# A decoder trunk on one core: the eight products of a weight tile in varying order

## The chip, the core and the metric

The kernel runs on one NeuronCore of a Trainium2 chip. TensorE (PE) multiplies; its weight loads (PEld) run beside its products. VectorE (DVE), ScalarE (ACT) and GpSimd (POOL) do elementwise work, SyncE (SP) issues most transfers. The metric is the device time of one execution in microseconds. Weights lie in HBM as float32. SBUF holds the tiles, PSUM (eight banks of 512 float32 columns by 128 partitions) the running sums.

## The reference

Two layers on 256 positions of width 2048, each a mixer and a gated MLP with a causal convolution, and a LayerNorm after each of them:

```python
h = x
mix = mamba2_mixer(h, mamba_w_in[0], ..., mamba_w_out[0])           # 2048 -> 10304, scan over 2 chunks, 4096 -> 2048
h = layer_norm(ALPHA * h + mix, ...)
h = layer_norm(ALPHA * h + conv_ffn(h, ffn_w_up[0], ..., ffn_w_down[0]), ...)   # 2048 -> 2 x 5632 -> 2048
k_blk, v_blk, k_mean = shared_kv(h, w_kv)                           # 2048 -> 4096
mix = moba_cross_attention(h, attn_w_q[0], attn_w_o[0], k_blk, v_blk, k_mean)   # 16 heads
h = layer_norm(ALPHA * h + mix, ...)
h = layer_norm(ALPHA * h + conv_ffn(h, ffn_w_up[1], ..., ffn_w_down[1]), ...)
```

Nearly all of the arithmetic is the products of the 256 positions with the large weight matrices. With 256 positions each weight is used for little work, so all weights pass through SBUF once.

## The kernel before

**Steps and chunks.** The weights are cut on the host into 881 tiles of 128 x 2 x 512 float32, half a megabyte each. One tile is one step (`steps`); a chunk (`Chunk`) is 512 columns of one weight matrix over its whole depth. The program is written out step by step at the end of `yoco_kernel`: for every step the functions hung before it, its products, then the functions hung after it. This order by hand sets the order on every engine.

**Two parts of each weight.** A float32 number is taken as the sum of a rounded part, `hi`, and the rest, `lo`, both in the type float32r. `split` (line 192) makes them: ACT casts the raw tile to `hi` (L223), DVE subtracts to get `lo` (L224), and then the load of a later tile is issued on SP's queue (L179). Four raw tiles and four tiles each of `hi` and `lo` exist. The activations are split in the same way: `hT` holds for each of 16 row blocks 256 columns of the high part and then 256 of the low one. `x.both(k)` is all 512, `x.hi(k)` the first 256.

**Where the tiles start.** `split` gives each kind of tile an offset in a row of `LINE` = 64 elements (lines 198 to 212). A plain `hi` tile has its two halves one right behind the other. A `hi` tile whose step is `behind` has 48 elements before its first half and 576 before its second. A `lo` tile of mode W has its halves 544 elements apart.

**Modes.** In mode W (560 steps: the Mamba input projection, most of both MLP up-projections, K and Q) the weights are TensorE's stationary operand, and the activations stream past them. In mode X (most of the rest) it is the other way round: the activations are stationary, the weights stream, and all products of a half of the positions add into one bank (`half`, L247, L248, L252); the last chunk of such a sum ends with products of 256 columns ("pieces"). One chunk has mode H (L289).

**The products of a W step** (`some`, line 258). A tile of a W chunk holds four row blocks of 256 columns. Its first index, `a`, is the part of the tile, `b` the row block within the part, `j` one of two 128-column pieces; numbered in the order (a, b, j), 0 to 3 lie in the first part and 4 to 7 in the second. `j` is also the PSUM bank that the product adds to. With p = 0 the weights are `hi` and 512 columns stream by (L275); with p = 1 they are `lo` and only the 256 high columns stream by (L278). In the first chunk of all a tile holds two row blocks of 512 columns, and `j` runs over four banks.

**Which comes first.** `whole` (line 293) issues the eight products of each kind. In the Mamba chunks each step has first one kind and then the other, and the next step begins with the kind that the last one ended with (`kinds`). In the others two steps are taken together: both with one kind, then both with the other. A step is `behind` (line 183) when its `hi` products follow `lo` products. The next tiles' splits are put into the stream after a fixed number of these products.

In the kernel before, the eight products with p = 0 go in the order 0 to 7, and the eight with p = 1 in the order 0, 1, 4, 5, 2, 3, 6, 7 (line 268). The first product of a bank in a chunk begins its sum, the last one ends it (`begins`, `ends`).

**Other work on TensorE.** L806 turns 128 x 128 tiles, L867 is a mean in two products of 256 columns, L823 and L832 belong to the scan.

Of the kernel before, what the change touches and what calls it, by code (L numbers as in the profile page):

```python
# [53 lines left out]
WARM0 = 18  # L54
HEAD, TAIL = 3, 4
LAST = 8
SPARE = 3


# [32 lines left out]
def yoco_kernel(ctx: ExitStack, tc: tile.TileContext, x, lmg, lmb, lfg, lfb, x_t, columns, w, out):  # L92
# [14 lines left out]
    def tp_tile():  # L107
        return psum.tile([P, NC], F32, tag="tp", name="tp", bufs=2)
# [73 lines left out]
    def behind(i):  # L182

        ch, s = steps[i]
        if ch.mode != "W" or (ch.paired and s % 2):
            return False
        if ch.kinds(s)[0] == 1:
            return True
        ch, s = steps[i - 1]
        return i > 0 and ch.mode == "W" and ch.kinds(s)[1] == 1  # L190
# [67 lines left out]
    def some(ch, s, p):  # L258

        i = ch.first + s  # L260
        nj = ch.nj
        w = ((hi_t, lo_t)[p][i]).rearrange("p a (k n) -> p a k n", n=nj * P)
        k0, half = ch.place(s)
        banks = [p[:, j, :] for p in ch.part[half:] for j in range(2)]
        first = ch.kinds(s)[0] == p
        order = [(a, b, j) for a in range(2) for b in range(ch.per // 2) for j in range(nj)]
        if p == 1:
            order = [order[i] for i in (0, 1, 4, 5, 2, 3, 6, 7)]
        for a, b, j in order:
            yield  # L270
            k = k0 + a * (ch.per // 2) + b
            begins, ends = first and k == 0, not first and k == ch.nk - 1
            js = slice(j * P, (j + 1) * P)
            if p == 0:
                nc.tensor.matmul(banks[j], w[:, a, b, js], ch.x.both(k), start=begins, stop=ends,  # L275
                                 skip_group_check=True)
            else:
                nc.tensor.matmul(banks[j][:, :S], w[:, a, b, js], ch.x.hi(k), start=begins, stop=ends,  # L278
                                 skip_group_check=True)
# [12 lines left out]
    def whole(i):  # L292

        ch, s = steps[i]
        if ch.mode == "H":
            return beside(i)
        a, b = ch.kinds(s)
        if not ch.paired:
            order = [(s, a), (s, b)]
        elif s % 2 == 0:  # L300
            order = [(s, a), (s + 1, a)]
        else:
            order = [(s - 1, b), (s, b)]
        late = ch.paired and s % 2
        n = len(order) * ch.per * ch.nj
        c = 0
        for t, p in order:
            for _ in some(ch, t, p):
                if c == (n // 2 if late else n * 3 // 8):
                    if late:  # L310
                        done(i - 1)
                    run(mid, i)
                    splits(i)
                c += 1
        if not ch.paired or late:
            done(i)

    def products(i):
# [6 lines left out]
        elif s == 0:  # L325
            a = acc_pair()
            ch.part = [a[:, 0, :], a[:, 1, :]] if ch.mode == "X" else [a]
            if ch.tail:
                if ch.tail == LAST:
                    ch.piece = [tp_tile()[:, :HC] for _ in range(2)]  # L330
# [49 lines left out]
    def beyond(i, t, q, f, *a):  # L380

        outer.setdefault((i, t, q), []).append((f, a))
# [168 lines left out]
    def summed(x, tail=TAIL):  # L551

        return [Chunk(Acts(x), tail=tail * (c == 3), head=2 * (c == 3)) for c in range(4)]

    def ffn_chunks(tail):
        return [(Chunk(hs, head=0 if j else HEAD), Chunk(hs)) for j in range(DFF // NC)], summed("g", tail)
# [7 lines left out]
    chA = summed("a")  # L564
    up1, down1 = ffn_chunks(LAST)
    n_steps = len(steps)
# [370 lines left out]
    def chain(norm, nxt=None, after=None):  # L937
# [16 lines left out]
        beyond(last, 1, 0, norm.scale, 0, 0)  # L954
        for e in range(SPARE):
            spare[last - SPARE + 1 + e] = 4 + 4 * e
        n = nxt.first
# [192 lines left out]
    for h in range(HEADS):  # L1150
        i, j = divmod(h, 4)
# [88 lines left out]
```

## Time and profile before

| | |
|---|---|
| median of two runs | 2505.25 us (2504.73 to 2505.77) |
| the profiled execution | 2505.77 us, its span 2503.5 us |
| clock granted to TensorE | 0.999 |
| TensorE busy | 2490.5 us, 99% of the span |
| weight loads busy | 2155.7 us, 86% |
| DVE, ACT, POOL busy | 1660.2, 1364.3, 76.4 us |
| DMA | 201 GB/s on average, 502.55 MB |

The span runs from the first instruction to the last; the time of the execution has some 2 us more around it. A product's recorded duration contains the time until its results are out and overlaps with the next product, so the pace of TensorE is read from the distance of starts, or from the lengths in the chain of waits, which follows the work that ended last back from the end and gives each piece its start, its length and the number of instructions in it.

### The profile page before, as it was taken

The page shows a single profiled execution, that of the slowest core. Times are in us where ns is not written, and L with a number is a line of the kernel's source. Part 1 is how long each engine was busy: PE and PEld are TensorE (multiplying, and loading weights), DVE is VectorE, ACT ScalarE, POOL GpSimd, SP SyncE. Part 2 cuts the span into 40 slices and gives each one's busy share as a digit, 9 for nine tenths or more (in the row PEclk, how much of TensorE's full clock was granted, in tenths as well). Part 3 has the DMA queues.
Part 4 walks back from the last instruction along what each step waited for, and adds up shares of the span by engine and source line. Part 5 has one row for each costly group of instructions (what it writes and reads, how often), then busy time and mean ns, then how long its engine had stood idle before and what let it go on. Part 6 is the DMA issues. An engine that isn't in the chain of part 4 may idle for free.

```text
span 2503.5 us, 35513 instructions
## 1 busy us (share of the span) xinstructions
PE 2490.5 (99%) x13695; PEld 2155.7 (86%) x13695; DVE 1660.2 (66%) x2144; ACT 1364.3 (54%) x1790; POOL 76.4 (3%) x96
## 2 busy tenths in 40 slices
PE   9999999999999999999999999999999999999998
PEld 8888888888888888888888888888888888888887
DVE  7778888855676767675445646645767676765545
ACT  6677787643465655554334445544556555554333
POOL 0000000000200000000000200000200000000001
PEclk9999999999999999999999999999999999999999
DMA  7666655666665555556676665457666555566675
GB/s 257 202 198 203 212 192 190 205 208 222 215 206 194 194 193 193 195 185 202 211 227 210 210 193 177 160 177 228 221 192 198 195 192 196 186 199 204 196 227 166
DMA packets 141738, 502.55 MB, mean 201 GB/s; under 512 B 15857, under 2 KB 16369, under 8 KB 141569
## 3 DMA queue, kind: packets, MB, share of 16 engines
q1 hardware_dynamic: 136448, 482.92, 59.0%
q0 software_dynamic: 4832, 16.85, 2.2%
q8 instruction: 107, 1.75, 0.3%
q14 instruction: 63, 0.51, 0.1%
q10 hardware_dynamic: 288, 0.52, 0.1%
HBM read 491.77 MB, written 8.45 MB: 200 GB/s over the span
## 4 chain that ended last, share of the span: by engine, by line
PE 98%; DMA 1%; DVE 0%; ACT 0%; issue 0%; SPq 0%; ACTq 0%; DVEq 0%
PE acc L275 41%; PE acc L278 20%; PE acc L247 11%; PE acc L252 11%; PE acc L248 11%; DMA raw<-in_w 1%; PE acc L823 1%; PE tp L419 0%; PE tp L832 0%; PE acc L806 0%; PE tp L1104 0%; PE tp L1138 0%; PE tp L1130 0%; PE tp L252 0%; PE tp L247 0%
## 5 line engine op out<-in xcount | busy, mean ns | idle before, releaser
L224 DVE TENSOR_TENSOR lo<-raw,hi 128x1024 fp32r<-128x1024 f32 (+1 forms) x869 | 1060.4, 1226 | 716.9 <-ACT hi L223 592.9
L223 ACT CAST hi<-raw 128x1024 fp32r<-128x1024 f32 (+1 forms) x869 | 907.9, 1048 | 822.1 <-PE acc L252 384.9
L275 PE MATMUL acc<-hT,hi 128*128 128x512 f32 x4480 | 1055.9, 391 | 1.2 <-ACT hi L223 1.2
L275 PEld LDWEIGHTS acc<-hT,hi 128*128 128x128 f32 x4480 | 826.6, 188 | 162.8 <-ACT hi L223 2.2
L278 PEld LDWEIGHTS acc<-hT,lo 128*128 128x128 f32 x4480 | 538.7, 188 | 15.6 <-issue 1.2
L278 PE MATMUL acc<-hT,lo 128*128 128x256 f32 x4480 | 544.4, 277 | 0.0
L247 PE MATMUL acc<-hi,gT 128*128 128x512 f32 (+1 forms) x670 | 260.5, 389 | 0.0
L248 PE MATMUL acc<-lo,gT 128*128 128x512 f32 (+1 forms) x670 | 260.3, 389 | 0.0
L252 PE MATMUL acc<-hi,gT 128*128 128x512 f32 (+1 forms) x670 | 206.0, 389 | 0.0
L248 PEld LDWEIGHTS acc<-lo,gT 128*128 128x128 f32 x670 | 125.8, 188 | 26.0
L247 PEld LDWEIGHTS acc<-hi,gT 128*128 128x128 f32 x670 | 125.8, 188 | 26.0 <-DVE r L473 0.3
L252 PEld LDWEIGHTS acc<-hi,gT 128*128 128x128 f32 x670 | 125.7, 188 | 25.9
L247 PE MATMUL acc<-hi,yT 128*128 128x512 f32 (+1 forms) x246 | 95.4, 388 | 0.0
L248 PE MATMUL acc<-lo,yT 128*128 128x512 f32 (+1 forms) x246 | 95.3, 388 | 0.0
L247 PE MATMUL acc<-hi,hT 128*128 128x512 f32 x192 | 78.8, 410 | 0.0
L248 PE MATMUL acc<-lo,hT 128*128 128x512 f32 x192 | 75.5, 393 | 0.0
L252 PE MATMUL acc<-hi,yT 128*128 128x512 f32 (+1 forms) x246 | 75.3, 388 | 0.0
L628 DVE TENSOR_TENSOR u<-u,acc 128x512 f32<-128x512 f32 x108 | 73.5, 682 | 2.4 <-ACT u L627 1.4
L655 DVE SCALAR_TENSOR_TENSOR g<-u,cols,g 128x254 f32<-128x254 f32 (+1 forms) x176 | 73.3, 478 | 2.1 <-ACT g L650 2.1
L1054 ACT CAST gT<-v 128x512 fp32r<-128x512 f32 x44 | 27.3, 621 | 84.6 <-DVE v L1053 84.6
L655 DVE SCALAR_TENSOR_TENSOR v<-u,cols,v 128x254 f32<-128x254 f32 (+1 forms) x176 | 73.1, 478 | 0.0
L486 POOL TENSOR_TENSOR rs<-rs,mhalf 128x1 f32<-128x1 f32 x8 | 7.4, 930 | 1975.5 <-DVE nb L487 1975.5
(224 smaller groups left out, 1824.7 us busy)
## 6 DMA issues: line engine op xcount, KB each, us to landing
raw<-in_w SPq DMA_DIRECT2D x880, 512.0 KB, 3.8
mA<-acum_d POOLq DMA_DIRECT2D x16, 512.0 KB, 6.7
hres<-r POOLq DMA_DIRECT2D x12, 512.0 KB, 7.1
r<-hres SPq DMA_DIRECT2D x12, 512.0 KB, 5.0
eA<-acum_d POOLq DMA_DIRECT2D x16, 128.0 KB, 7.9
r<-in_x SPq DMA_DIRECT2D x4, 512.0 KB, 5.5
gb<-in_ln_mix_g SPq DMA_DIRECT2D x8, 256.0 KB, 4.9
gb<-in_ln_mix_b SPq DMA_DIRECT2D x8, 256.0 KB, 5.1
```

Source lines behind the costliest of these rows:

```text
L223: nc.scalar.copy(h[:, sl], t[:, sl])
L224: nc.vector.tensor_sub(l[:, sl], t[:, sl], h[:, sl].bitcast(F32))
L247: nc.tensor.matmul(a, th, h[:, kk, sl], start=k == k0, stop=False)
L248: nc.tensor.matmul(a, th, l[:, kk, sl], start=False, stop=False)
L252: nc.tensor.matmul(a, ch.x.lo(k)[:, ts], h[:, kk, sl], start=False, stop=k == k1 - 1)
L275: nc.tensor.matmul(banks[j], w[:, a, b, js], ch.x.both(k), start=begins, stop=ends, skip_group_check=True)
L278: nc.tensor.matmul(banks[j][:, :S], w[:, a, b, js], ch.x.hi(k), start=begins, stop=ends, skip_group_check=True)
L486: nc.gpsimd.tensor_tensor(self.rs[:, h, :], self.rs[:, h, :], mhalf[:, 0, :], op=OP.pow)
L628: nc.vector.tensor_add(dst, dst, p[:, :, :S])
L655: nc.vector.scalar_tensor_tensor(d, u[:, i % 2, :S - k], c1(self.at_w, w[n - 1 - k] + self.ia + i), d, op0=OP.mult, op1=OP.add)
L823: nc.tensor.matmul(ps[64 * q:64 * q + 64, c, j * P:(j + 1) * P], G[g]["xdt"][:, c, h * 64:(h + 1) * 64], G[g]["A", c][:, h, :], start=True ...
L1054: nc.scalar.copy(h, v[:, sl])
```

## The change

Instead of one order, a step's eight products take one of several. For p = 1, in every W step, it is one of ten; for p = 0, in the steps that are `behind` and are not the first tile of their chunk, one of nine; the other p = 0 steps keep 0 to 7. Which one it is follows from the number of the step, multiplied by a constant, shifted and taken modulo the number of orders, so that it looks random and is the same in each run. In all of them 0, 1, 2, 3 come in this sequence among themselves, and so do 4, 5, 6, 7. `begins` and `ends` are now worked out from the place in the order, so that a bank's first and last product in a chunk carry them.

```diff
+TURNS = (((0, 1, 2, 3, 4, 5, 6, 7), (0, 4, 5, 6, 7, 1, 2, 3), (0, 1, 4, 5, 6, 7, 2, 3), (0, 1, 2, 4, 5, 6, 7, 3),
+          (0, 4, 1, 5, 2, 6, 3, 7), (4, 0, 1, 2, 3, 5, 6, 7), (4, 0, 5, 1, 6, 2, 7, 3), (0, 1, 4, 5, 2, 3, 6, 7),
+          (4, 5, 6, 7, 0, 1, 2, 3)),
+         ((0, 1, 4, 5, 2, 3, 6, 7), (0, 4, 1, 5, 2, 6, 3, 7), (0, 4, 5, 1, 2, 6, 7, 3), (0, 4, 5, 6, 7, 1, 2, 3),
+          (4, 0, 5, 1, 6, 2, 7, 3), (4, 0, 1, 5, 6, 2, 3, 7), (4, 0, 1, 2, 3, 5, 6, 7), (0, 1, 4, 2, 5, 3, 6, 7),
+          (0, 1, 2, 4, 5, 6, 3, 7), (4, 5, 6, 0, 1, 2, 3, 7)))
...
         order = [(a, b, j) for a in range(2) for b in range(ch.per // 2) for j in range(nj)]
-        if p == 1:
-            order = [order[i] for i in (0, 1, 4, 5, 2, 3, 6, 7)]
-        for a, b, j in order:
+        if p == 1 or (behind(i) and s):
+            turns = TURNS[p]
+            order = [order[m] for m in turns[(i * 2654435761 >> 9) % len(turns)]]
+        for m, (a, b, j) in enumerate(order):
             yield
             k = k0 + a * (ch.per // 2) + b
-            begins, ends = first and k == 0, not first and k == ch.nk - 1
+            js = [n for n, o in enumerate(order) if o[2] == j]
+            begins = first and k0 == 0 and m == js[0]
+            ends = not first and k0 + ch.per == ch.nk and m == js[-1]
```

## The prediction

> **What bounds the kernel now.** I read the page first, then the chain of waits in three stretches, then single products in the timeline. The page says how full TensorE is and who stands on the chain that ended last:
>
> ```profile
> span 2503.5 us, 35513 instructions
> PE 2490.5 (99%) x13695; PEld 2155.7 (86%) x13695; DVE 1660.2 (66%) x2144; ACT 1364.3 (54%) x1790; POOL 76.4 (3%) x96
> ...
> PE 98%; DMA 1%; DVE 0%; ACT 0%; issue 0%; SPq 0%; ACTq 0%; DVEq 0%
> PE acc L275 41%; PE acc L278 20%; PE acc L247 11%; PE acc L252 11%; PE acc L248 11%; DMA raw<-in_w 1%; PE acc L823 1%; PE tp L419 0%; PE tp L832 0%; PE acc L806 0%; PE tp L1104 0%; PE tp L1138 0%; PE tp L1130 0%; PE tp L252 0%; PE tp L247 0%
> ```
>
> TensorE carries 98% of the chain, and the two lines that the diff reorders, L275 (512 columns, "wide") and L278 (256 columns, "narrow"), carry 61% of it. The other engines have idle time, so only TensorE's own pace counts. The groups of instructions say whether these two lines ever wait, and the table of cores gives the clock:
>
> ```profile
> L275 PE MATMUL acc<-hT,hi 128*128 128x512 f32 x4480 | 1055.9, 391 | 1.2 <-ACT hi L223 1.2
> L278 PE MATMUL acc<-hT,lo 128*128 128x256 f32 x4480 | 544.4, 277 | 0.0
> ...
> core 0: 2503.5 us, clock 0.999
> ```
>
> 4480 products of each kind, 1.2 us of idle time before them in total, and the clock granted in full (0.999). The mean of one (391 and 277 ns) contains a pipeline's latency; the pace is the distance from one product to the next, which the chain gives (start, length, what). First a stretch where two tiles go together, then one where each goes alone:
>
> ```profile
> 915.03 7.26 PE acc L275 x32
> 922.29 3.63 PE acc L278 x32
> 925.92 7.26 PE acc L275 x32
> 933.18 3.63 PE acc L278 x32
> ...
> 254.35 3.63 PE acc L275 x16
> 257.99 1.82 PE acc L278 x16
> 259.81 3.63 PE acc L275 x16
> 263.44 1.82 PE acc L278 x16
> ```
>
> A wide product takes 7.26/32 = 0.2269 us and a narrow one 3.63/32 = 0.1134 us, the half of it to the nanosecond; in the lone tiles it is 0.2269 and 0.1138. Nothing lies between the pieces: each begins where the last one ends. 4480 x (0.2269 + 0.1134) = 1524.5 us, and 61% of the span is 1527 us. So these products already run at one even pace, and no wait is left in them for an order to remove. What a new order can do is to change the pace itself.
>
> **The change part by part.** No product, load, split or wait is added or removed; inside a step of eight, the products come in another sequence, and each part's own four stay in their order. Which sequence a step takes follows from its number by the formula in the diff, so I wrote all of them out and counted.
>
> *Narrow products.* All 560 steps draw one of ten orders; 55 draw the present one, so 505 steps, 4040 products, change. *Wide products.* 183 steps are turned (those whose wide products follow narrow ones, the first tile of a chunk left out); 20 draw the present order, so 163 steps, 1304 products, change. The first product and the last of each bank keep the flags that start and end a sum.
>
> What differs between neighbours then: (a) Now two neighbours in a step never write the same PSUM bank. After, 1446 neighbouring pairs of narrow products and 285 of wide ones do. (b) Now narrow products change the part of the tile after every second one. After, a part comes up to six times in a row: 494 products are the third of such a run, 292 the fourth or later. (c) 61 wide steps begin with the second part of the tile, not the first.
>
> *(a), wide.* In the summing chunks every run of products writes one bank, L247, L248 and L252 alike:
>
> ```profile
> 1200.30 0.39 PE L247 MATMUL acc<-hi,gT 128*128 128x512 f32 x1
> ...
> 1200.52 0.39 PE L248 MATMUL acc<-lo,gT 128*128 128x512 f32 x1
> ...
> 1200.75 0.39 PE L247 MATMUL acc<-hi,gT 128*128 128x512 f32 x1
> ...
> 1200.98 0.39 PE L248 MATMUL acc<-lo,gT 128*128 128x512 f32 x1
> ```
>
> They start 0.68/3 = 0.227 us apart, as the wide ones of the W tiles do. 285 pairs cost nothing.
>
> *(a), narrow.* Two rows bear on it, and they differ. The first is the pair of L867, two narrow products into one bank (chain, then the next piece's start); the second are the narrow products of a summing chunk's tail, again all into one bank:
>
> ```profile
> 266.92 0.40 PE L867 MATMUL tp<-sq,mean 128*128 128x256 f32 x2
> 267.15 0.61 PE L754 MATMUL tp<-CT,BT 128*128 128x128 f32 x4
> ...
> 2488.36 0.28 PE L247 MATMUL tp<-hi,gT 128*128 128x256 f32 x1
> 2488.48 0.28 PE L248 MATMUL tp<-lo,gT 128*128 128x256 f32 x1
> 2488.60 0.28 PE L247 MATMUL tp<-hi,gT 128*128 128x256 f32 x1
> 2488.72 0.28 PE L248 MATMUL tp<-lo,gT 128*128 128x256 f32 x1
> 2488.84 0.40 PE L252 MATMUL tp<-hi,gT 128*128 128x256 f32 x2
> 2489.08 0.28 PE L247 MATMUL tp<-hi,gT 128*128 128x256 f32 x1
> ```
>
> L867's two take 0.23 us, so at least one is near 0.11; the tail's take 0.12 each (0.72 for six). If a shared bank were the cause of 0.120, both of L867 could not fit well into 0.23, and the wide rows would show 6.6 ns more too. I take nothing, and keep 0.120 - 0.1134 = 6.6 ns as the upper end: 1446 x 6.6 = 9.5 us.
>
> *(b).* The tail's 0.120 has another candidate: the weight load. Each product brings its own load of 128 columns, which runs beside the product before it. Beside a wide one there is time to spare; beside a narrow one hardly. In the tail, weights and stream start at the same offset within a row of 64 elements; the code gives the narrow weights of a W tile other offsets, and its two parts two different ones (lines 198 to 212). No row shows what a long run of one part does. Ends: nothing, and 6.6 ns for each product from the third of a run on, 786 x 6.6 = 5.2 us. The rows of present runs of two (0.1134) are nearest; I take 2 ns for the 786 within these ends, 1.6 us.
>
> *(c).* The second part of such a wide tile has the plain offset, as in the tail. Its first weight load runs beside the last narrow product, so I give it 6.6 ns: 61 x 6.6 = 0.4 us. The other loads of wide products lie beside products of 0.227 us, about twice the tail's 0.120, and are hidden.
>
> *The start.* Only the first two tiles are split part by part, and step 1 draws (0, 1, 2, 4, 5, 6, 7, 3): its first product of the second part comes one place earlier.
>
> ```profile
> 9.82 1.14 ACT L223 CAST hi<-raw 128x512 fp32r<-128x512 f32 x2 [0.63 <-DMA raw<-in_w]
> ...
> 10.49 2.13 PE L275 MATMUL acc<-hT,hi 128*128 128x512 f32 x8 [1.19 <-ACT hi L223]
> ```
>
> Both casts are done at 10.96 us; three products after 10.49 it is 11.17 at the earliest. The cover holds; without it, it would be some 0.2 us once. Later tiles are split in one piece, so any order waits alike. The last narrow or wide product of a step still frees its tile, and the places where splits are put into the stream (after so many products) stay, so DVE, ACT and the DMA queues see the same times.
>
> Sum: 0 + 1.6 + 0.4 = 2.0 us. The profiled execution took 2505.77 us (its span of 2503.5 and 2.3 around it), half a microsecond above the median of the runs shown, 2505.25. From the median: **2507 us**. About 2%, some 50 us, is what a measurement of this kernel can tell from no change.
>
> A rule that speaks against every cost above stands in the Trainium skill, "TensorE: Matmul & The Clock Gate", section "Step-by-step: what each phase is for": the array reads weights and stream through two independent ports, so a weight load takes nothing from the running product. By it (b) and (c) would be zero and the sum 0 to 9.5 us. The tail's 0.120 against 0.1134 for the same 256 columns shows that something beside the columns counts, so I don't follow the rule to the end.
>
> **The rivals.** *The shared bank costs.* Price 6.6 ns on 1446 pairs and on nothing else: 2505.3 + 0.4 + 9.5 = 2515 us. The tail's rows speak for it, L867 and the wide rows against.
>
> *Slower: weight loads come out from behind the narrow products.* Place: L278, whose loads have the least room. Price between 5.2 us (only runs of three and more) and, if the strict alternation by twos is what keeps the pace, 4040 x 6.6 = 26.7 us: 2511 to 2532. For it speaks that the parts' offsets differ and that 0.120 exists at all; against it that the present stream, which crosses between parts on every second product and between all four corners of the tile, shows no product out of line. It makes the kernel slower by over 2% only from 50.1/4040 = 12.4 ns per changed product on, twice what the tail pays, or if the wide ones suffer too: 1304 would then have to pay some 18 ns each beside the 6.6.
>
> *Faster: the present pace is not a floor.* A weight load of the same 128 columns goes with a short product in less time:
>
> ```profile
> 284.39 0.87 PE acc L806 x8
> ```
>
> 0.87/8 = 0.109 us. If the even narrow pace of 0.1134 contains a collision between load and stream that other sequences avoid, 4040 x 4.4 ns = 17.8 us go: 2488 us. Against it: all 4480 stand at the same value in both stretches, whichever part or bank they have, and exactly half of a wide one, where loads have time to spare; a pace in proportion to the columns is not the mark of loads. The Trainium skill ("TensorE: Matmul & The Clock Gate", "Back-to-back issue gap") has columns/2.4 + 2.5 ns, an estimate of 109 ns for 256 columns and 216 for 512, and by it there would be room. No row of these lines here comes down to it.
>
> *The change does not act*, since the order is not what TensorE sees: then 2505, not to be told from the forecast.
>
> **How the numbers follow.** Forecast (no cost or a few us, 2503 to 2510, with the case that it doesn't act): 0.60. Shared bank, 2515: 0.10. Weight loads, 2511 to 2532: 0.17, of which 0.04 are for a price beyond every row, above 2555. Faster, 2488 to 2503: 0.13, with 0.01 below 2455. The range 2496 to 2525 leaves out the lower half of the faster case (0.07) and the upper part of the slower one (0.08), and 8 in 10 remain. Over 2% faster 0.01, within 2% 0.95, slower 0.04.
>
> **What would show it.** In the profile after, the chain's runs of L275 x32 should stay at 7.26 us and those of L278 x32 at 3.63 to 3.66; L275 and L278 keep 41% and 20% of the chain, and the waits of ACT and DVE stay as they are. A shared bank shows as narrow products of 0.120 exactly where two neighbours have one bank (means by order differ); weight loads show in runs of one part, growing with the run, and in the mean of L278 rising from 277 ns towards the tail's 283. Runs of 3.5 us would be the faster case. Wrong I would be most easily where a sequence sets off something that no row of before contains, above all in the 1304 wide products, to which I gave no cost of their own.

## The result and the profile after

2517.95 us (2517.78 to 2518.11) against 2505.25 us: the ratio is 1.0051, 95% interval 1.0035 to 1.0067. The change costs 12.7 us between the medians and 12.0 between the two profiled executions (2505.77 and 2517.78). The page after, with the rows that answer to those of before (the two product lines are now L285 and L288, the splits L230 and L231):

```profile
span 2515.5 us, 35513 instructions
PE 2501.9 (99%) x13695; PEld 2163.1 (86%) x13695; DVE 1659.6 (66%) x2144; ACT 1364.9 (54%) x1790; POOL 76.4 (3%) x96
...
PE 99%; DMA 0%; DVE 0%; issue 0%; ACT 0%; SPq 0%; ACTq 0%; DVEq 0%
PE acc L285 41%; PE acc L288 21%; PE acc L254 11%; PE acc L255 11%; PE acc L259 11%; PE acc L833 1%; DMA raw<-in_w 0%; PE tp L429 0%; PE tp L842 0%; PE acc L816 0%; PE tp L1114 0%; PE tp L1148 0%; PE tp L1140 0%; PE tp L259 0%; PE tp L255 0%
...
L285 PE MATMUL acc<-hT,hi 128*128 128x512 f32 x4480 | 1060.3, 391 | 1.3 <-ACT hi L230 1.3
...
L288 PE MATMUL acc<-hT,lo 128*128 128x256 f32 x4480 | 551.8, 278 | 0.0
```

The instructions are the same in number, DVE, ACT and POOL are as busy as before, and the two lines wait no more than they did (1.3 us and nothing). TensorE's busy time grew by 11.4 us. The chain of waits in a stretch of the first MLP (start, length, what) shows where; before, each piece of 32 wide products had 7.26 us and each of 32 narrow ones 3.63:

```profile
917.70 3.65 PE acc L288 x32
921.35 7.26 PE acc L285 x32
928.61 3.65 PE acc L288 x32
932.26 7.30 PE acc L285 x32
939.56 3.73 PE acc L288 x32
943.28 7.26 PE acc L285 x32
950.54 3.64 PE acc L288 x32
954.18 7.28 PE acc L285 x32
```

The pieces still join without a gap, but most are longer, by differing amounts: the pace changed, no wait came. Taking the distance from the start of each product to the start of the next in the trace and adding over all 4480 of a kind gives 1021.7 us wide and 513.5 narrow before, 1026.4 and 520.8 after: +4.7 and +7.3, the whole of the difference between the two spans. All other products took 956.7 us in both, and the clock is 0.999 in both.

The same distances speak on the bank at once. In the trace after, a narrow product whose successor writes the same bank takes 115.5 ns on average (1441 of them), one whose successor writes the other bank takes 115.6 within a part (1910) and 115.2 across parts (913); 17 pairs more than 200 ns apart are left out. And within one order the eight distances are nearly the same from step to step where the step before them is of the same kind. For 0, 4, 1, 5, 2, 6, 3, 7 right after wide products they are 119, 117, 122, 118, 114, 119, 118, 120 ns; for its mirror 4, 0, 5, 1, 6, 2, 7, 3 they are 118, 116, 114 and then five times 113 (medians). So the loss is in some orders and not in others, and it is not noise.

### The profile page after: what moved, and what is told of

Its sections match the earlier page's. It is cut to its first block, busy times and chain, and to the rows that moved or that the text cites. A ratio compares the mean times of both kernels' runs of the same rounds, so it can differ in the third digit from the quotient of the medians.

```text
span 2515.5 us, 35513 instructions
## 1 busy us (share of the span) xinstructions
PE 2501.9 (99%) x13695; PEld 2163.1 (86%) x13695; DVE 1659.6 (66%) x2144; ACT 1364.9 (54%) x1790; POOL 76.4 (3%) x96
## 4 chain that ended last, share of the span: by engine, by line
PE 99%; DMA 0%; DVE 0%; issue 0%; ACT 0%; SPq 0%; ACTq 0%; DVEq 0%
PE acc L285 41%; PE acc L288 21%; PE acc L254 11%; PE acc L255 11%; PE acc L259 11%; PE acc L833 1%; DMA raw<-in_w 0%; PE tp L429 0%; PE tp L842 0%; PE acc L816 0%; PE tp L1114 0%; PE tp L1148 0%; PE tp L1140 0%; PE tp L259 0%; PE tp L255 0%
## 5 line engine op out<-in xcount | busy, mean ns | idle before, releaser
L231 DVE TENSOR_TENSOR lo<-raw,hi 128x1024 fp32r<-128x1024 f32 (+1 forms) x869 | 1059.8, 1225 | 727.4 <-ACT hi L230 597.7
L230 ACT CAST hi<-raw 128x1024 fp32r<-128x1024 f32 (+1 forms) x869 | 908.8, 1048 | 832.5 <-PE acc L259 385.9
L285 PE MATMUL acc<-hT,hi 128*128 128x512 f32 x4480 | 1060.3, 391 | 1.3 <-ACT hi L230 1.3
L285 PEld LDWEIGHTS acc<-hT,hi 128*128 128x128 f32 x4480 | 826.9, 188 | 167.1 <-ACT hi L230 2.4
L288 PEld LDWEIGHTS acc<-hT,lo 128*128 128x128 f32 x4480 | 545.6, 188 | 15.6 <-issue 1.2
L288 PE MATMUL acc<-hT,lo 128*128 128x256 f32 x4480 | 551.8, 278 | 0.0
```

Source lines behind the costliest of these rows:

```text
L230: nc.scalar.copy(h[:, sl], t[:, sl])
L231: nc.vector.tensor_sub(l[:, sl], t[:, sl], h[:, sl].bitcast(F32))
```

## The experiments

My theory at this point: what counts is the sequence of the weights' start offsets. `split` places the two halves of a narrow tile, and of a wide tile that is `behind`, at different offsets in a row of 64 elements. In the program as built, the stream and the plain wide tiles start at 32, the halves of a narrow tile at 16 and 48, those of a `behind` tile at 16 and 32. A reordered step loads weights from another sequence of these. Rivals: the order of the products as such (a shared bank, jumps of the stream between row blocks), and the variation itself, each step differing from the last.

### One kind at a time

```diff
# lo_only
-        if p == 1 or (behind(i) and s):
+        if p == 1:
# hi_only
-            turns = TURNS[p]
+            turns = TURNS[p][:1] if p else TURNS[0]
```

> Only the narrow products take the ten orders; the wide ones all keep 0 to 7. In the profile after, the narrow products account for 7.3 of the 12 us and the wide ones for 4.7. If the two shares stand by themselves, 2505.3 + 7.3 = 2513 us. If the wide products' loss comes from the state in which reordered narrow ones leave TensorE, nearly all of it comes back here: 2516 to 2518. If the narrow ones lose only because of reordered wide ones ahead of them, 2506.

> Only the wide products of the steps behind narrow ones take the nine orders; the narrow ones all keep 0, 1, 4, 5, 2, 3, 6, 7. Shares that stand by themselves: 2505.3 + 4.7 = 2510 us, and the narrow products stay at 513.5 us in sum. If the wide orders cost nothing by themselves: 2505 to 2506. The bank theory prices 285 shared banks here at nothing or at 6.6 ns, 1.9 us at most: 2507.

Measured: narrow alone 2514.13 us, ratio 1.0035 (1.0022 to 1.0048); wide alone 2509.17, ratio 1.0015 (1.0005 to 1.0024). The two losses, 8.5 and 3.5 us against the runs of before that were measured beside them, add up to about the whole. In sums of distances, narrow products alone cost 6.5 us at their own line and 0.8 at the wide ones; wide ones alone 3.2 at theirs and nothing at the narrow ones. These sums differ by some 1 us between runs, but single steps show that the 0.8 is real. In lo_only, whose wide products all go 0 to 7, 153 `behind` tiles begin a run of several wide tiles right after narrow ones. In 126 of them the eight products take 1820 ns, as before; 27 take 1831 to 1857, and these are exactly the ones that follow a narrow product of over 114 ns among the last two. Each kind loses for itself, with a little that narrow products pass on.

### Both halves at one offset

```diff
# even_before from before, even_after from after: the same two lines
-                h = h[:, LINE // 2:].rearrange("p (a n) -> p a n", a=2)[:, :, LINE // 4:]
+                h = h[:, LINE * 3 // 4:LINE * 3 // 4 + 2 * NC].rearrange("p (a n) -> p a n", a=2)
...
-                l = l.rearrange("p (a n) -> p a n", a=2)[:, :, :NC]
+                l = l[:, :2 * NC].rearrange("p (a n) -> p a n", a=2)
```

> The kernel before, but the two halves of a narrow tile start at the same offset in a row of 64 elements, and so do the halves of a wide tile that is behind (both at the first half's offset). Its orders are those of before. It is the base for the next run. The theory of offsets (a weight load takes longer where it follows one of another offset, or is in step with the stream) doesn't say on which side of 2505 it lies: if both halves stand well to the stream by themselves, 2505; if the alternation of two offsets is what keeps the pace, up to 2505 + 30.

> The same equal offsets with the varying orders of after. Theory of offsets: with both halves at one offset, the order of the parts no longer changes the sequence of offsets, so this is within 2 us of the run before it (even_before). Theory of order itself (jumps in the stream's row blocks, a bank written twice in a row): it is some 12 us slower than even_before, as after is than before. Theory of the shared bank alone: 9 us slower, all in narrow products with 0.120 us where neighbours share a bank.

All loads of a narrow tile and of a `behind` tile now start at 16, beside a stream that stays at 32. Measured: 2528.17 us with the old orders (1.009, 1.0075 to 1.0105) and 2528.50 with the varying ones (1.0092, 1.0077 to 1.0107). The chain in the same stretch, first with the orders of before:

```profile
920.06 3.77 PE acc L278 x32
923.83 7.30 PE acc L275 x32
931.12 3.77 PE acc L278 x32
934.89 7.30 PE acc L275 x32
```

and with the varying orders:

```profile
919.62 3.77 PE acc L288 x32
923.38 7.30 PE acc L285 x32
930.68 3.77 PE acc L288 x32
934.45 7.30 PE acc L285 x32
```

The two are alike to the hundredth: 3.77/32 = 117.8 ns for a narrow product, whatever the order. Over the whole kernel the sums of distances are 530.2 and 530.0 us narrow, 1026.6 and 1026.1 wide. All that the change reorders (banks, row blocks, the change from step to step) is still in even_after, and it costs nothing once the halves have one offset. A small cost could hide beneath this slower pace; the single orders below answer that at the pace of before. The runs also show what the two offsets are worth: 2528.2 - 2505.3 = 23 us, of which 16.7 are in the narrow line and 4.9 in the wide one.

### One order at a time

```diff
# by_chunk
         if p == 1 or (behind(i) and s):
+            q = ch.first // 8 if (i < 600) == (p == 1) else 0
             turns = TURNS[p]
-            order = [order[m] for m in turns[(i * 2654435761 >> 9) % len(turns)]]
+            order = [order[m] for m in turns[q % len(turns)]]
```

> Narrow products up to step 600: one order through a whole chunk, the ten in turn from chunk to chunk, wide ones 0 to 7. From step 600 on: the nine wide orders, one through a whole chunk, narrow ones as before. Theory of the sequence of offsets: each order then has a pace of its own in the steps whose predecessor has the same order; orders that alternate the parts by ones or twos without a break (0, 4, 1, 5, ...; 4, 0, 5, 1, ...; 0, 1, 4, 5, ...) stand near 0.1134 us, and those with runs of three or four towards 0.1177, the pace with one offset. Theory of the mix (only the change of the order from step to step costs): all ten stand at 0.1134 to 0.1138 inside a chunk.

One execution, 2511.39 us, against a median of 2505.32 us before. What it was for is a table from its trace: the time of a step's eight narrow products, in ns (medians), where four narrow steps follow one another: in the step right after wide products, in the next one, and in the third and fourth, by when the stream has settled. The second column gives the part, 0 or 1, that each product loads from.

| order | parts | after wide | next | third |
|---|---|---|---|---|
| 0,1,4,5,2,3,6,7 | 00110011 | 914 | 907 | 907 |
| 4,0,5,1,6,2,7,3 | 10101010 | 914 | 907 | 907 |
| 0,1,4,2,5,3,6,7 | 00101011 | 914 | 907 | 907 |
| 4,0,1,2,3,5,6,7 | 10000111 | 927 | 907 | 907 |
| 4,0,1,5,6,2,3,7 | 10011001 | 940 | 934 | 907 |
| 4,5,6,0,1,2,3,7 | 11100001 | 940 | 921 | 907 |
| 0,4,5,6,7,1,2,3 | 01111000 | 943 | 925 | 907 |
| 0,4,1,5,2,6,3,7 | 01010101 | 945 | 922 | 907 |
| 0,1,2,4,5,6,3,7 | 00011101 | 949 | 918 | 907 |
| 0,4,5,1,2,6,7,3 | 01101001 | 947 | 947 | 947 |

Neither expectation holds as I wrote it. The orders do have times of their own, but runs of one part are not what makes them: 1, 0, 0, 0, 0, 1, 1, 1 settles at 907, which is 113.3 ns a product, and the strict alternation 0, 1, 0, 1, ... is among the slow ones after wide products while its mirror is among the fastest. Nine orders hold 113.3 once there; they differ in how long they take to get there after wide products. The tenth never does. There is a state: the same order takes 945 or 907 ns by what went before.

From step 600 on the same trace has the nine wide orders, each through a whole chunk. Right after narrow products, the eight products of a `behind` step take 1820 ns for 0 to 7 and for 0, 4, 5, 6, 7, 1, 2, 3; the others take 1826 to 1857. The dearest is 0, 1, 4, 5, 2, 3, 6, 7, one of the three orders in which narrow products settle fastest. So no order is good by itself; the offsets that it meets differ between the two kinds of tile (16 and 48, 16 and 32).

### Wide tiles at the plain offset

```diff
# plain_hi_before from before, plain_hi_after from after
-                h = h[:, LINE // 2:].rearrange("p (a n) -> p a n", a=2)[:, :, LINE // 4:]
+                h = h[:, LINE:LINE + 2 * NC].rearrange("p (a n) -> p a n", a=2)
```

> The kernel before, but the wide tiles that are behind take the plain offset for both halves. By the prediction's step (c) the first weight load of such a tile then costs 6.6 ns beside the last narrow product, 183 x 6.6 = 1.2 us, and the other wide products fall to 0.2267: some 8 ns less in each of these steps, 1.5 us. Together 2505 us, within 1.5. If plain offsets make the first load much dearer (say 20 ns): 2508.

> The varying orders with plain offsets for both halves of every wide tile; narrow tiles keep their two offsets. Theory of offsets: the wide orders then cost nothing, the wide products stand as in plain_hi_before, and what is left is the narrow products' loss: plain_hi_before + 7.5 to 8.5 us, about 2513 to 2514. Theory that the wide orders cost by themselves (stream or bank): 2516 to 2518.

Measured: 2508.51 us (1.0013, 1.0003 to 1.0022) and 2515.80 us (1.0042, 1.0028 to 1.0056). The difference of 7.3 us is about the narrow products' loss that was expected (7.5 to 8.5), and the wide ones make none by their order (1024.3 and 1024.7 us in sums of distances): all nine orders take 1840 ns for the eight products, 233, 236, 228, 233, 231 and then 227 three times. But the level was not what I expected. With 16 and 32, 0 to 7 takes 1820 ns; with 32 for both, 1840. A `behind` tile whose weights are all in step with the stream costs 20 ns more, spread over its first five products, not 6.6 on one; 184 such tiles make 3.7 us, about the 3.2 measured against the runs of before measured beside it. Which of its loads costs the first nanoseconds isn't shown apart.

### One narrow order for the whole kernel

```diff
# all_40516273; likewise all_04152637, all_04512673, all_45016723
-            order = [order[i] for i in (0, 1, 4, 5, 2, 3, 6, 7)]
+            order = [order[i] for i in (4, 0, 5, 1, 6, 2, 7, 3)]
```

> The kernel before with one narrow order for all steps: 4, 0, 5, 1, 6, 2, 7, 3. It changes the part after every product and puts four of seven neighbouring pairs into one bank, 2240 pairs less those of the first chunk. If an order is dear only by the sequence of offsets, and this one finds back to 0.1134 us after wide products as it did in by_chunk: 2505 to 2506.5. If varying the order is what costs, the same. If shared banks cost 6.6 ns: 2505 + 14 = 2519.

> The mirror of it for all steps: 0, 4, 1, 5, 2, 6, 3, 7, with the same number of changes and of shared banks. By the sequence of offsets as by_chunk showed it, the first narrow step after wide ones takes 0.945 in place of 0.914 us and some of the next step follows: 176 x 0.031 + 176 x 0.018 = 8.6 us, 2514. If the number of changes or of shared banks decides: the same as the run before it.

> 0, 4, 5, 1, 2, 6, 7, 3 for all steps. In by_chunk it never came back to 0.1134: 0.9467 us for each step, whatever stood before it. So 184 x 0.0325 + 376 x 0.040 = 21 us, 2526. If varying the order from step to step is what costs, it is at 2505 to 2506, since nothing varies.

> 4, 5, 0, 1, 6, 7, 2, 3 for all steps, the order of before with its parts exchanged; none of the runs so far had it. No theory here gives its value; since the two offsets lie at equal distance on both sides of the stream's, one would expect about the time of before, 2503 to 2508. Under 2503 it would beat both kernels.

Measured, in this order: 2505.62 us, ratio 1.0001 (0.9992 to 1.0011); 2513.62, 1.0031 (1.0019 to 1.0044); 2528.82, 1.0093 (1.0078 to 1.0108); 2508.60, 1.0014 (1.0005 to 1.0024). The first two have the same number of changes of part and of shared banks, over two thousand pairs each, and differ by 8 us; the third has fewer changes and the most loss. Chains of the first and the third in the same stretch:

```profile
921.30 3.63 PE acc L278 x32
924.94 7.26 PE acc L275 x32
932.20 3.63 PE acc L278 x32
935.83 7.26 PE acc L275 x32
```

```profile
920.28 3.79 PE acc L278 x32
924.07 7.28 PE acc L275 x32
931.35 3.79 PE acc L278 x32
935.13 7.28 PE acc L275 x32
```

3.63 us is the pace of before, with a shared bank at every second product; 3.79 is dearer than equal offsets (3.77), with nothing varying. In the third kernel the wide products lose too (7.28), although their order is 0 to 7: they follow narrow ones that are not settled, and a `behind` step takes 1841 ns in place of 1820. Three expectations worked out from the table (2505 to 2506.5, 2514, 2526) came in at 2505.6, 2513.6 and 2528.8; the third was low by 2.8 us. The table did not contain the wide products, whose line took 1024.2 us in sums of distances against 1021.7 of before (+2.5); the narrow line took 532.0 against 513.5 (+18.5, where the table gave 21), so the agreement is better in the sum than in its parts. For the fourth there was no theory, only 2503 to 2508, and it came in just above.

### The offsets exchanged, the order kept

```diff
# swapped
-                l = l.rearrange("p (a n) -> p a n", a=2)[:, :, :NC]
+                l = l.rearrange("p (a n) -> p a n", a=2)[:, :, LINE // 2:]
```

> The kernel before with its own orders, 0, 1, 4, 5, 2, 3, 6, 7 and 0 to 7; only the two offsets of a narrow tile's halves are exchanged, so that the first half has the offset of the second and the other way round. If nothing but the sequence of offsets counts, this is all_45016723 again: 2508 to 2509, the first narrow step after wide ones at 0.934 us and all the others at 0.907. If the halves count for another reason (their products, row blocks or banks), it is at 2505 to 2506, as before.

Measured: 2508.54 us, 1.0014 (1.0004 to 1.0023). Its chain, and then that of all_45016723, which exchanges the parts in the order and not in memory:

```profile
923.33 3.65 PE acc L278 x32
926.99 7.26 PE acc L275 x32
934.24 3.65 PE acc L278 x32
937.90 7.26 PE acc L275 x32
```

```profile
923.28 3.65 PE acc L278 x32
926.93 7.26 PE acc L275 x32
934.19 3.65 PE acc L278 x32
937.85 7.26 PE acc L275 x32
```

The two kernels agree to 1 ns even in single products: after wide ones both take 118, 118, 117, 124, 116, 114, 113, 113 ns (medians), where the kernel before takes 117, 116, 114 and then 113. Swapped has the order, the banks and the row blocks of before, and costs 3.4 us more by the placement alone. In this pair, an order of the parts and a placement of the parts are the same thing to TensorE: a sequence of offsets.

## Why the prediction was right and wrong

The time, 2518, lies in the range of 2496 to 2525 and within 2%; the forecast of 2507 was low by 11 us. That is in part luck: the case to which I gave 0.60, no cost or a few us (2503 to 2510), did not come, and the range holds the time because it was widened for the rivals. I also took 2%, some 50 us, as the least that a measurement can tell from no change; the interval of this result, 1.0035 to 1.0067, tells 12.7 us from none. Step by step:

- **What bounds the kernel**: right. TensorE's own pace and nothing else; no wait came or went, and the loss is in L285 and L288 alone.
- **Part (a), the bank**: right for both widths. The pair of L867 was the row to believe; in all_40516273 over two thousand shared banks cost nothing that can be measured (ratio 1.0001). The rival at 2515, near the measured time as it is, has the wrong mechanism. Of the two candidates for the tail's 0.120 the bank is thus out; its weights and its stream both start at 32, which fits the other one, but no run moved them apart.
- **Part (b), the narrow weight loads**: the right place and too low. I took 2 ns for 786 products, 1.6 us; the narrow line lost 7.3 us, and the kernel with narrow orders alone lost 8.5. What failed is the rule by which I counted: that a product pays from the third of a run on. Strict alternation pays after wide products and a run of four does not, once settled; it is the whole sequence and what stands before it. The upper price, 26.7 us for all changed products, was of the right size: 23 us with one offset and 23 with the dearest order tried, of which 16.7 and 18.5 in the narrow line.
- **Part (c) and "the other loads of wide products ... are hidden"**: wrong, and the second miss. I gave 0.4 us; the wide line lost 4.7, and the kernel with wide orders alone lost 3.5. Wide products pay as well, up to 236 ns in place of 227, although their loads have twice the time. The prediction's last sentence named this as the likeliest place to be wrong. The trace of before had the sign of it: the first four of a `behind` step stand 226, 229, 232 and 227 ns apart, and I had put the three extra ones down to the passage from narrow to wide, without giving them a term.
- **The start**: right. The first two pieces of eight wide products in the chain take 2.12 and 2.08 us, against 2.13 and 2.09 before.
- **The rule on two ports** that spoke against every cost (the Trainium skill, "TensorE: Matmul & The Clock Gate", "Step-by-step: what each phase is for"): what I drew from it, that a weight load costs the product beside it nothing, does not hold here. The kernels before and even_before differ only in where weights lie, and by 23 us, while a load's recorded time is 188 ns in both. Whether a port has to do with it, no row shows.
- **The rivals**: "slower" had the mechanism nearest to the truth, at 2511 to 2532, with a chance of 0.17. I let the present rows, which show one sequence of offsets only, count as evidence that any sequence would do. "Faster": no sequence in any run took a settled narrow product below 113 ns, so the present pace is a floor for what can be done by order and offset as tried here.

What the sum missed is all of one kind, the pace under another sequence of offsets: 4.7 + 7.3 = 12 us in place of 2.0.

What stays open is why a given sequence settles or not. The offsets and the order explain which kernel is fast, and the table foretells the time of others, but no row shows the inside of the load or the stream. Why 1, 0, 1, 0, ... settles in three products after wide ones and 0, 1, 0, 1, ... doesn't in eight wasn't found out. Other offsets than 16, 32 and 48 in 64 weren't tried, and the stream stayed at 32 in all runs.

## What to carry to other kernels

Where every product brings its own weight load, the start addresses of successive weight tiles can belong to the schedule, as they do here for 256 and for 512 columns: before reordering products, write down the sequence of their offsets against the stream, and keep the sequence that the measured pace belongs to. A steady pace in a trace proves its own sequence only, not the others. A cheap test of whether an order matters by itself is to give all weight tiles the same offset and reorder again; to exchange two offsets under an unchanged order is the test from the other side.

## What was unexpected of the hardware

- The same narrow product takes 113.3 ns, 117.8 ns or, in the dearest order tried, 118.4 ns (3.79/32) by the offsets of the weights loaded around it, with no wait shown and the clock at 0.998 to 0.999.
- The pace has a memory across instructions: the order 0, 4, 1, 5, 2, 6, 3, 7 takes 945 ns for eight right after wide products and 907 once settled, and unsettled narrow products slow the wide ones after them, 1841 ns in place of 1820.
- With equal offsets in a tile, nine orders of the wide products agree to within some 2 ns in 1840, and two kernels with wholly different orders to within 0.4 us in 2528.
